# MLP second product: gate and residual applied to finished row blocks, first contributions copied by ScalarE

## The chip, the cores and the metric

The kernel runs on one core of a Trainium2 chip. The metric is the device time of one execution in microseconds (us). The engines are TensorE (PE, with its weight loads PEld), VectorE (DVE), ScalarE (ACT), GpSimd (POOL) and SyncE (SP), whose queue issues every DMA of this kernel. SBUF is the working memory of 128 partitions, PSUM the memory that TensorE writes its products to.

## The reference

One decoder layer over 2048 rows of width 1024, in float32. The last third is what matters here:

```
x = layer_norm(ALPHA * x + gt1 * y, ln1_g, ln1_b)
h = x * (1.0 + sc2) + sh2
f = square(relu(h @ w_ff1)) @ w_ff2          # 1024 -> 4096 -> 1024
x = layer_norm(ALPHA * x + gt2 * f, ln2_g, ln2_b)
```

`gt2` is one row of 1024 numbers (the gate), so `gt2 * f` scales the columns of `f`. `ALPHA * x` is the residual of the MLP.

## The kernel before

A scheduler orders the instructions of each engine when the program is built; on the chip every engine works through its own queue in that fixed order and waits where an input is late. Products in float32 are made of three passes over a high and a low part of each operand: `split` writes the high part with ScalarE and the low part (`x - high`) with VectorE, mostly; `mm3` issues three matmuls.

The stages that the change touches, with their place in the profile:

- **Output projection** (about 1080 to 1300 us). For each of 16 row tiles of 128 rows, `z` is normalised by ScalarE; then GpSimd makes `x2 = z * ag1 + ab1` in two instructions of 128x1024 (L1003, L1004), where `ag1` and `ab1` are ALPHA times the gain and bias of the first norm. `x2`, the residual, is stored to HBM (`ax2_d`).
- **First product** (about 1290 to 2002 us). Two halves of 1024 rows, 16 column blocks each. `split_h` makes seven operands of a half (Strassen's seven products P1 to P7; h, hh, hl in the profile; L1058 are its subtractions, on VectorE and GpSimd). In between, `prep` prepares `w_ff2` for the second product 16 times: load, multiply by the gate (two VectorE instructions of 128x1024, L1129), differences, split into w2s, store to `wt_d`.
- **Second product** (about 2002 us to the end). `down(half, s)` runs for two halves and four slices `s` of the inner dimension, seven products of 48 matmuls each. A half has eight row tiles, `acc[0]` to `acc[7]`. Before, `acc[t]` is loaded with the residual `x2` and every product is added to it by VectorE from PSUM (L1252). The products accumulate in PSUM banks W, Z and X (d_W, d_Z, d_X).
- **`finish(half, t)`** makes the second layer norm of a row tile: statistics (VectorE), 1/std (GpSimd, in `rs`), normalise (ScalarE), times `g2` (GpSimd), plus `b2` (GpSimd or VectorE), store. In the second half tiles 3, 5, 6 and 7 do it on VectorE alone with scalar_tensor_tensor (L1191, L1194). The eight `finish` of the first half run beside the first slice of the second half; those of the second half are the end of the program. In the last slice the order of products is P1, P5, P6, P3, P2, P7, P4; tiles 0 to 3 are finished after P2, tiles 4 to 7 after P4.

Of the kernel before, what the change touches and what calls it, by code (L numbers as in the profile page):

```python
# [10 lines left out]
F32 = mybir.dt.float32  # L11
# [105 lines left out]
def build(nc, tc, I, out, upto=9, dbg=None):  # L117
# [17 lines left out]
    ax2_d = tc.dram_tile((NT, P, D), F32, name="ax2_d")  # L135
# [12 lines left out]
    dbg.update(ax2=ax2_d, h=h_d, mix=mix_d, h2=h2_d, qn=qn_d, qr=qr_d, kn=kn_d, kr=kr_d, v=v_d, gt=gt_d)  # L148
# [785 lines left out]
    c3b = pool(p3, "c3b")  # L934
# [21 lines left out]
    ag0, ab0, ag1, ab1 = (p.tile([P, D], F32, name=n) for p, n in ((c3, "ag0"), (c3, "ab0"), (c3b, "ag1"), (c3b, "ab1")))  # L956
    for t, n in ((ag0, "ln_in_g"), (ab0, "ln_in_b"), (ag1, "ln1_g"), (ab1, "ln1_b")):
        rowbc(t, I[n])
        G.tensor_scalar(t, t, ALPHA, 0.0, op0=OP.mult, op1=OP.add)
# [12 lines left out]
    for b in border:  # L972
        xns = []
        for tp in range(2):
# [149 lines left out]
    def prep(u):  # L1124
# [3 lines left out]
        for i in range(2):  # L1128
            V.tensor_tensor(b[:, i], b[:, i], gt2, op=OP.mult)  # L1129
# [47 lines left out]
    g2 = c4.tile([P, D], F32, name="g2")  # L1177
    b2 = c4.tile([P, D], F32, name="b2")
    rowbc(g2, I["ln2_g"])
    rowbc(b2, I["ln2_b"])  # L1180
# [22 lines left out]
    def down(half, s, n):  # L1203
# [13 lines left out]
        def prod(x, name, ch, start, src, subs, *adds):  # L1217
# [62 lines left out]
    def load_acc(half, t):  # L1280
        acc[t] = acs[t].tile([P, D], F32, tag="c", name=f"acc{half}_{t}")
        with tc.issue_after(wdma[-1]):
            Q.dma_start(acc[t], ax2_d[4 * border[2 * half + t // 4] + t % 4])
# [56 lines left out]
```

## Time and profile before

| | |
|---|---|
| Three runs | 2644.70, 2646.72, 2647.34 us; median 2646.72 |
| The profiled execution | 2645.24 us, of which the span from first to last instruction is 2643.5 us and 1.7 us lie around it |
| Busy, share of the span | PE 93%, PEld 77%, DVE 68%, ACT 45%, POOL 43% |
| Granted TensorE clock, mean | 0.97 of 2.4 GHz |

A busy share is an average over stages with different limits; what a change is worth in one stage is read from that stage. A matmul of 128x512 starts 0.226 us after the one before it where TensorE runs without a gap at full clock (220 us held 972 of them between 2370 and 2590 us), so the count of matmuls in a stretch tells how much of it TensorE lost, be it by waiting or by a lower clock.

### The profile page before, as it was taken

How to read it: one execution, taken by the hardware profiler on the slowest of the kernel's cores; microseconds unless marked ns; L12 is line 12 of the kernel's file. 1: busy time of each engine (PE TensorE's matmuls, PEld its weight loads, DVE VectorE, ACT ScalarE, POOL GpSimd, SP SyncE). 2: the span in 40 equal slices, each digit the busy share in tenths (PEclk: the TensorE clock that was granted, in tenths of full speed). 3: DMA queues.
4: the chain of work that ended last, by engine and by line, in shares of the span. 5: the costliest groups of instructions: out<-in, count | busy, mean ns of one | idle time of the engine just before them, and what ended most of it. 6: DMA issues, size and time to landing. Idle time of an engine off the chain costs nothing.

```text
span 2643.5 us, 33756 instructions
## 1 busy us (share of the span) xinstructions
PE 2457.8 (93%) x11668; PEld 2028.1 (77%) x11668; DVE 1809.5 (68%) x2919; ACT 1188.1 (45%) x2317; POOL 1126.6 (43%) x1055
## 2 busy tenths in 40 slices
PE   6999999989999999899789999799999999999997
PEld 5887778877787878677577778677788888878885
DVE  8757675565767676766887755978645665776657
ACT  4653222246777777433455555455553111221111
POOL 4323545547978888577722223532220000330004
PEclk9999999988999999999889999899999999999998
DMA  9456341021112020655278863578838766776653
GB/s 327 146 196 224 108 133 50 31 73 32 48 37 61 20 62 13 219 183 192 104 263 268 280 229 107 174 255 278 293 123 349 271 245 256 295 301 244 225 191 127
DMA packets 194251, 464.69 MB, mean 176 GB/s; under 512 B 17560, under 2 KB 51736, under 8 KB 179744
## 3 DMA queue, kind: packets, MB, share of 16 engines
q1 hardware_dynamic: 194080, 462.54, 50.3%
q8 instruction: 92, 1.51, 0.2%
q14 instruction: 79, 0.65, 0.1%
HBM read 313.30 MB, written 149.17 MB: 175 GB/s over the span
## 4 chain that ended last, share of the span: by engine, by line
PE 54%; DVE 16%; DMA 13%; issue 6%; POOL 6%; ACT 5%; SPq 1%; DVEq 0%; ACTq 0%; POOLq 0%
DMA wt_d<-w2s 5%; PE d_W L131 4%; PE d_W L133 4%; PE d_W L132 4%; PE t L834 3%; DMA wad<-in_w_ada 2%; PE pj L133 2%; PE pj L132 2%; PE pj L131 2%; PE d_Z L132 2%; PE d_Z L133 2%; PE d_Z L131 2%; PE o L827 2%; PE o L825 2%; PE s L131 2%
## 5 line engine op out<-in xcount | busy, mean ns | idle before, releaser
L180 POOL TENSOR_SCALAR rs<-mv 128x1 f32<-128x1 f32 x32 | 16.0, 503 | 607.4 <-DVE mv L190 607.0
L128 DVE TENSOR_TENSOR w1l_P<-w,w1h_P 128x512 fp32r<-128x512 f32 x224 | 187.7, 844 | 69.4 <-ACT w1h_P L125 68.8
L806 ACT ACTIVATE p<-s,nm 128x512 f32<-128x512 f32 (+3 forms) x320 | 196.4, 627 | 41.8 <-DVE nm L803 38.3
L801 DVE TENSOR_REDUCE mx<-s 128x1 f32<-128x512 f32 (+3 forms) x288 | 175.0, 619 | 55.9 <-PE s L133 53.1
L1074 POOL TENSOR_TENSOR w<-w 128x512 f32<-128x512 f32 x56 | 81.7, 1463 | 286.7 <-DMA w<-in_w_ff 214.6
L125 ACT ACTIVATE w1h_P<-w 128x512 fp32r<-128x512 f32 x224 | 136.9, 622 | 108.2 <-PE u_Y L132 26.8
L850 POOL TENSOR_TENSOR tl<-tf,th 128x512 fp32r<-128x512 f32 x144 | 184.4, 1292 | 1.7
L834 PE MATMUL t<-ident,p 128*128 128x128 f32 x1088 | 164.3, 276 | 5.6 <-ACT tf L845 1.9
L834 PEld LDWEIGHTS t<-ident,p 128*128 128x128 f32 x1088 | 130.6, 142 | 30.8 <-ACT tf L845 6.1
L131 PE MATMUL pj<-wbh,hhb 128*128 128x512 f32 x384 | 151.3, 396 | 0.9 <-ACT wbh L125 0.5
L133 PE MATMUL pj<-wbh,hlb 128*128 128x512 f32 x384 | 152.1, 397 | 0.0
L132 PE MATMUL pj<-wbl,hhb 128*128 128x512 f32 x384 | 151.9, 396 | 0.2 <-DVE wbl L128 0.2
L131 PE MATMUL s<-kt,qt 96*128 96x512 f32 (+3 forms) x320 | 130.4, 408 | 11.5 <-ACT p L806 9.7
L1074 POOL TENSOR_TENSOR w<-w,w 128x512 f32<-128x512 f32 x56 | 81.8, 1461 | 133.8 <-DVE w1l_P L128 132.2
L128 DVE TENSOR_TENSOR w2s<-w2r,w2s 128x512 fp32r<-128x512 f32 x112 | 92.1, 825 | 66.8 <-ACT w2s L125 66.5
L125 ACT ACTIVATE w2s<-w2r 128x512 fp32r<-128x512 f32 x112 | 70.2, 628 | 146.0 <-DMA wt_d<-w2s 123.0
L827 PE MATMUL o<-tl,v 128*128 128x512 f32 (+2 forms) x320 | 123.3, 394 | 7.1 <-DVE tl L128 4.8
L825 PE MATMUL o<-th,v 128*128 128x512 f32 (+2 forms) x320 | 121.9, 385 | 5.6 <-DVE osum L861 4.5
L132 PE MATMUL s<-kt,qt 96*128 96x512 f32 (+3 forms) x320 | 120.4, 376 | 3.7 <-DVE kt L128 3.7
L133 PE MATMUL s<-kt,qt 96*128 96x512 f32 (+3 forms) x320 | 120.1, 376 | 0.0
L131 PE MATMUL u_W<-hh_P,w1h_P 128*128 128x512 f32 x256 | 102.6, 401 | 15.8 <-ACT hh_P L125 6.5
L133 PE MATMUL u_X<-hh_P,w1l_P 128*128 128x512 f32 x256 | 104.1, 408 | 12.4 <-DVE w1l_P L128 12.3
(372 smaller groups left out, 7850.6 us busy)
## 6 DMA issues: line engine op xcount, KB each, us to landing
wP<-wt_d SPq DMA_DIRECT2D x112, 1024.0 KB, 4.8
wt_d<-w2s SPq DMA_DIRECT2D x112, 512.0 KB, 4.9
w<-in_w_ff SPq DMA_DIRECT2D x64, 512.0 KB, 5.2
a<-g_d SPq DMA_DIRECT2D x32, 1024.0 KB, 6.3
g_d<-v SPq DMA_DIRECT2D x96, 256.0 KB, 4.2
wad<-in_w_ada SPq DMA_DIRECT2D x64, 256.0 KB, 2.9
w2r<-in_w_ff SPq DMA_DIRECT2D x16, 1024.0 KB, 7.7
x<-in_x SPq DMA_DIRECT2D x16, 512.0 KB, 8.2
```

What stands on the lines that cost most here:

```text
L125: A.activation(hi, x, AF.Copy)
L128: lo_eng.tensor_tensor(lo, x, hi.bitcast(F32), op=OP.subtract)
L131: T.matmul(ps, sh, mh, start=start, stop=False, skip_group_check=more)
L132: T.matmul(ps, sh, ml, start=False, stop=False, skip_group_check=more)
L133: T.matmul(ps, sl, mh, start=False, stop=stop, skip_group_check=more)
L801: V.tensor_reduce(mx[:, j:j + 1], ps[:, :n], op=OP.max, axis=AX.X)
L806: A.activation(pt[:, :m], b[:, :m], AF.Exp, bias=nm, accum_out=rs[:, qi, j:j + 1])
L825: T.matmul(po[:, cs], w, th[:, cs], start=(done == 0), stop=False)
L827: T.matmul(po[:, cs], w, tl[:, cs], start=False, stop=(done == nk))
L834: T.transpose(tp[:, qi * P:(qi + 1) * P], pts[h, 4 * qb + qi, kb // 4][1][:, kb % 4 * P:(kb % 4 + 1) * P], ident)
L850: (V if mode == "C" else G).tensor_tensor(tl[:, cs], tf[:, cs], th[:, cs].bitcast(F32), op=OP.subtract)
L1074: (V if half == 0 and c < W1V else G).tensor_tensor(src, *sub, op=op)
```

## The change

- `prep` no longer multiplies `w_ff2` by the gate. The gate and the residual are applied when a row tile is complete: `gate` multiplies `acc[t]` by `gt2` and adds the residual `zt`, two VectorE instructions of 128x1024 a tile.
- The output projection stores `z` itself (to `z_d`) and leaves out L1003 and L1004. `residual` loads `z` again for each of the 16 tiles, into a pool `ztp` of two slots, and GpSimd makes `z * ag1 + ab1` there, two instructions of 128x1024 a tile.
- With no residual in it at the start, `acc[t]` is no longer loaded. Its first contributions (P1, P5, P6 and P4 of slice 0) are written by ScalarE copies from PSUM; 32 VectorE adds and 16 loads go.
- In the last slice of the second half the gate of tiles 4 to 7 comes ahead of P4, and P4's own part is gated apart: `y = W * gt2`, `acc += y`, two VectorE instructions of 128x512 a tile. `y` takes a slot of `ztp`.
- `acc[0]` to `acc[3]` have one buffer in place of two. `gt2`, `ag1`, `ab1`, `g2` and `b2` are loaded in the second product, after slice 1.

```diff
-                    x2 = x3.tile([P, D], F32, tag="x2", name=f"x2_{tt}")
-                    G.tensor_tensor(x2, z, ag1, op=OP.mult)
-                    G.tensor_tensor(x2, x2, ab1, op=OP.add)
-                    Q.dma_start(ax2_d[tt], x2)
+                    Q.dma_start(z_d[tt], z)
...
-        for i in range(2):
-            V.tensor_tensor(b[:, i], b[:, i], gt2, op=OP.mult)
...
-    acs = [pool(p4b, f"ac{t}", 2) for t in range(8)]
+    acs = [pool(p4b, f"ac{t}", 1 if t < 4 else 2) for t in range(8)]
...
+    ztp = pool(p4b, "ztp", 2)
...
+    def residual(half, t):
+        zt = ztp.tile([P, D], F32, tag="zt", name=f"zt{half}_{t}")
+        with tc.issue_after(wdma[-1]):
+            Q.dma_start(zt, z_d[4 * border[2 * half + t // 4] + t % 4])
+        G.tensor_tensor(zt, zt, ag1, op=OP.mult)
+        G.tensor_tensor(zt, zt, ab1, op=OP.add)
+        return zt
+
+    def gate(f, zt):
+        V.tensor_tensor(f, f, gt2, op=OP.mult)
+        V.tensor_tensor(f, f, zt, op=OP.add)
 
     def finish(half, t):
         tt = 4 * border[2 * half + t // 4] + t % 4
         f = acc[t]
+        if half == 0 or t < 4:
+            gate(f, residual(half, t))
...
             if half == 1 and last and name == "P4":
                 ops = [parts(q) for q in range(2)]
                 for tp in range(4):
+                    gate(acc[4 + tp], residual(half, 4 + tp))
+                for tp in range(4):
                     for k in range(4):
                         mm(tp, k, *ops[k // 2])
+                    y = ztp.tile([P, D], F32, tag="zt", name=f"y{tp}")[:, 0:512]
+                    V.tensor_tensor(y, ps[ch, tp], gt2[:, 0:512], op=OP.mult)
+                    V.tensor_tensor(acc[4 + tp][:, 0:512], acc[4 + tp][:, 0:512], y, op=OP.add)
+                return
...
                     if s == 0 and name in ("P1", "P5"):
-                        load_acc(half, 4 * i + tp)
+                        acc[4 * i + tp] = acs[4 * i + tp].tile([P, D], F32, tag="c", name=f"acc{half}_{4 * i + tp}")
                     c = acc[4 * i + tp][:, 512 * j:512 * j + 512]
-                    V.tensor_tensor(c, c, ps[ch, tp], op=OP.add)
+                    if s == 0 and name in ("P1", "P5", "P6", "P4"):
+                        A.activation(c, ps[ch, tp], AF.Copy)
+                    else:
+                        V.tensor_tensor(c, c, ps[ch, tp], op=OP.add)
```

**GpSimd's queue at the start of the first product.** `h4_0_01` and `h4_0_00` are operands of `split_h`, `x2_2` and `x2_3` the residuals of the last two row tiles. Before:

```order
L1003 TENSOR_TENSOR x2_2_14679<-z2_14577,ag1_13258 128x1024
L1058 TENSOR_TENSOR h4_0_01_14849<-h4_0_11_14851,h4_0_01_14849 128x1024
L1004 TENSOR_TENSOR x2_2_14679<-x2_2_14679,ab1_13259 128x1024
L1003 TENSOR_TENSOR x2_3_14720<-z3_14589,ag1_13258 128x1024
L1058 TENSOR_TENSOR h4_0_00_14847<-h4_0_01_14849,h4_0_00_14847 128x1024
L1004 TENSOR_TENSOR x2_3_14720<-x2_3_14720,ab1_13259 128x1024
L1058 TENSOR_TENSOR h4_0_01_14849<-h4_0_10_14853,h4_0_01_14849 128x1024
L128 TENSOR_TENSOR hl0_P2_14886<-h4_0_10_14853,hh0_P2_14885 128x1024
```

And of the changed kernel, the same place:

```order
L1051 TENSOR_TENSOR h4_0_01_14786<-h4_0_11_14788,h4_0_01_14786 128x1024
L1051 TENSOR_TENSOR h4_0_00_14784<-h4_0_01_14786,h4_0_00_14784 128x1024
L1051 TENSOR_TENSOR h4_0_01_14786<-h4_0_10_14790,h4_0_01_14786 128x1024
L128 TENSOR_TENSOR hl0_P7_14815<-h4_0_00_14784,hh0_P7_14814 128x1024
L128 TENSOR_TENSOR hl0_P2_14823<-h4_0_10_14790,hh0_P2_14822 128x1024
```

The three subtractions stand one behind the other; the four residual instructions among and ahead of them are gone.

**VectorE's queue where the first half is finished** (after P2 of its last slice; gP7l and gP4l are low parts that TensorE waits for). Before:

```order
L1252 TENSOR_TENSOR acc0_0_20392<-acc0_0_20392,d0_3_X0_22044 128x512
L188 BN_STATS st_22112<-acc0_0_20392 128x6
L188 BN_STATS st_22126<-acc0_1_20395 128x6
L190 BN_AGGR mv_22115<-st_22112 128x2
L199 TENSOR_SCALAR nm_22118<-mv_22115,rs_22117 128x1
L128 TENSOR_TENSOR gP7l0_3_1_22201<-a4_0_3_00_21764,gP7h0_3_1_22200 128x1024
L1252 TENSOR_TENSOR acc0_1_20395<-acc0_1_20395,d0_3_X1_22045 128x512
```

Of the changed kernel:

```order
L1187 TENSOR_TENSOR acc0_2_20305<-acc0_2_20305,gt2_20224 128x1024
L128 TENSOR_TENSOR gP4l0_3_0_22167<-a4_0_3_11_21674,gP4h0_3_0_22166 128x1024
L1188 TENSOR_TENSOR acc0_1_20303<-acc0_1_20303,zt0_1_22040 128x1024
L1187 TENSOR_TENSOR acc0_3_20307<-acc0_3_20307,gt2_20224 128x1024
L1188 TENSOR_TENSOR acc0_2_20305<-acc0_2_20305,zt0_2_22060 128x1024
```

Between the low parts stand a multiplication by `gt2` and an addition of `zt` for each tile, and the addition waits for GpSimd's `zt`.

**GpSimd's queue at the end of the program**, from the norm of tile 1 of the second half. Before:

```order
L1199 TENSOR_TENSOR acc1_1_22427<-acc1_1_22427,g2_20316 128x1024
L1199 TENSOR_TENSOR acc1_2_22430<-acc1_2_22430,g2_20316 128x1024
L1200 TENSOR_TENSOR acc1_2_22430<-acc1_2_22430,b2_20317 128x1024
L180 TENSOR_SCALAR rs_24333<-mv_24331 128x1
L181 TENSOR_TENSOR rs_24333<-rs_24333,mhalf_115 128x1
```

Of the changed kernel:

```order
L1182 TENSOR_TENSOR zt1_5_24254<-zt1_5_24254,ag1_20225 128x1024
L180 TENSOR_SCALAR rs4_24163<-mv_24161 128x1
L1183 TENSOR_TENSOR zt1_5_24254<-zt1_5_24254,ab1_20226 128x1024
L181 TENSOR_TENSOR rs4_24163<-rs4_24163,mhalf_115 128x1
L1209 TENSOR_TENSOR acc1_1_22382<-acc1_1_22382,g2_20227 128x1024
L1209 TENSOR_TENSOR acc1_2_22384<-acc1_2_22384,g2_20227 128x1024
L1182 TENSOR_TENSOR zt1_6_24260<-zt1_6_24260,ag1_20225 128x1024
L1182 TENSOR_TENSOR zt1_7_24266<-zt1_7_24266,ag1_20225 128x1024
L1210 TENSOR_TENSOR acc1_2_22384<-acc1_2_22384,b2_20228 128x1024
L1183 TENSOR_TENSOR zt1_6_24260<-zt1_6_24260,ab1_20226 128x1024
L1183 TENSOR_TENSOR zt1_7_24266<-zt1_7_24266,ab1_20226 128x1024
```

The residuals of tiles 5 to 7 stand among the norms of tiles 1 and 2; `zt1_7` is the last of them.

## Rows read from the trace of the kernel before

**Rows 1.** The page: busy us, share of the span, instructions of two engines.
```profile
PE 2457.8 (93%) x11668; PEld 2028.1 (77%) x11668; DVE 1809.5 (68%) x2919; ACT 1188.1 (45%) x2317; POOL 1126.6 (43%) x1055
```

**Rows 2.** Stretches: length, busy PE, PEld, DVE, ACT, POOL (count), clock, DMA share, GB/s.
```profile
1290.00:1340.00 50.00, 27.57 (x90) 20.75 (x89) 41.94 (x34) 24.04 (x30) 34.71 (x15) 0.66 0.36 132
1340.00:1640.00 300.00, 284.14 (x1207) 229.37 (x1206) 206.10 (x284) 163.76 (x288) 72.05 (x51) 0.98 0.70 233
1640.00:1705.00 65.00, 51.37 (x193) 39.62 (x192) 62.76 (x46) 33.08 (x50) 43.97 (x18) 0.87 0.43 138
1705.00:2000.00 295.00, 283.56 (x1217) 228.92 (x1216) 199.56 (x270) 162.37 (x285) 78.88 (x55) 0.99 0.70 237
2270.00:2370.00 100.00, 93.69 (x404) 76.44 (x403) 83.64 (x95) 26.80 (x25) 43.82 (x28) 0.98 0.83 313
2370.00:2590.00 220.00, 220.00 (x972) 182.19 (x971) 131.43 (x147) 43.54 (x41) 0.00 (x0) 1.00 0.60 221
2590.00:2644.00 54.00, 33.68 (x138) 27.02 (x136) 44.45 (x60) 8.17 (x7) 27.47 (x23) 0.84 0.30 115
```

**Rows 3.** What PE waited for, 1290 to 1345 us: total, times, longest.
```profile
PE u_Y L132 <- DVE hl_P L128: 10.0, 2, 7.3
PE u_W L131 <- ACT hh_P L125: 6.5, 1, 6.5
```

**Rows 4.** GpSimd in order of time, 1290 to 1345 us: start, length, instruction.
```profile
1299.20 2.38 POOL L1003 TENSOR_TENSOR x<-z,ag 128x1024 f32<-128x1024 f32 x1
...
1318.80 2.37 POOL L1058 TENSOR_TENSOR h<-h,h 128x1024 f32<-128x1024 f32 x1 [2.35 <-issue]
```

**Rows 5.** VectorE at the second `split_h`: two gate multiplications in a row.
```profile
1681.59 5.65 DVE L1129 TENSOR_TENSOR w2r<-w2r,gt 128x1024 f32<-128x1024 f32 x2
```

**Rows 6.** ScalarE at the same place: idle time before the instruction, in brackets.
```profile
1685.05 0.63 ACT L125 ACTIVATE w2s<-w2r 128x512 fp32r<-128x512 f32 x1 [6.04 <-DVE w2r L1129]
```

**Rows 7.** All gate multiplications of `prep`: duration ns min/median/max, first and last.
```profile
L1129 DVE TENSOR_TENSOR w2r<-w2r,gt x32: 1211/1218/3423, 1333.4 to 1815.6; 128x1024 f32<-128x1024 f32 x32
```

**Rows 8.** What ScalarE waited for, 1330 to 1900 us.
```profile
ACT w2s L125 <- DMA wt_d<-w2s: 123.0, 67, 5.3
```

**Rows 9.** Adds from PSUM and statistics on `acc`: duration ns min/median/max.
```profile
L1252 DVE TENSOR_TENSOR acc<-acc,d_W x128: 628/686/690, 2011.9 to 2633.6; 128x512 f32<-128x512 f32 x128
L188 DVE BATCH_NORM_STATS2 st<-acc x32: 636/680/695, 2274.3 to 2634.3; 128x6 f32<-128x512 f32 x32
```

**Rows 10.** VectorE where the first half is finished, in order of time.
```profile
2277.77 0.69 DVE L1252 TENSOR_TENSOR acc<-acc,d_X 128x512 f32<-128x512 f32 x1 [0.47 <-PE d_X L133]
...
2297.10 3.41 DVE L1200 TENSOR_TENSOR acc<-acc,b 128x1024 f32<-128x1024 f32 x1 [0.35 <-POOL acc L1199]
...
2322.63 1.87 DVE L188 BATCH_NORM_STATS2 st<-acc 128x6 f32<-128x512 f32 x3
2324.42 1.20 DVE L1200 TENSOR_TENSOR acc<-acc,b 128x1024 f32<-128x1024 f32 x1
2325.54 1.21 DVE L1223 TENSOR_TENSOR a<-a,a 128x1024 f32<-128x1024 f32 x1
...
2366.31 1.23 DVE L128 TENSOR_TENSOR gP2l<-a,gP2h 128x1024 fp32r<-128x1024 f32 x1 [4.21 <-ACT gP2h L125]
```

**Rows 11.** GpSimd at the same place.
```profile
2282.46 2.40 POOL L1199 TENSOR_TENSOR acc<-acc,g 128x1024 f32<-128x1024 f32 x1 [1.61 <-ACT acc L1198]
...
2294.64 8.12 POOL L1199 TENSOR_TENSOR acc<-acc,g 128x1024 f32<-128x1024 f32 x3
```

**Rows 12.** VectorE at the end of the program: first and last instruction.
```profile
2591.20 0.69 DVE L1252 TENSOR_TENSOR acc<-acc,d_X 128x512 f32<-128x512 f32 x1 [0.47 <-PE d_X L133]
...
2638.98 1.41 DVE L1194 SCALAR_TENSOR_TENSOR acc<-acc,rs,b 128x512 f32<-128x512 f32 x2
```

**Rows 13.** DMA issues: KB each, median us from issue to landing.
```profile
axl<-in_x SPq DMA_DIRECT2D x16, 512.0 KB, 4.4
```

**Rows 14.** A ScalarE copy from PSUM: duration ns min/median/max.
```profile
L1100 ACT ACTIVATE u<-u_X x31: 574/578/587, 1337.9 to 1986.7; 128x512 f32<-128x512 f32 x31
```

More of the change, by code (lines that the diff above doesn't have):

```diff
@@ L133, in mm3 @@
         T.matmul(ps, sl, mh, start=False, stop=stop, skip_group_check=more)
-    ax2_d = tc.dram_tile((NT, P, D), F32, name="ax2_d")
+    z_d = tc.dram_tile((NT, P, D), F32, name="z_d")
     h_d = [tc.dram_tile((4, P, KD, P), F32, name=f"h_d{b}") for b in range(NB)]
@@ L147, in build @@
     gt_d = [tc.dram_tile((1, D), F32, name=f"gt_d{i}") for i in range(2)]
-    dbg.update(ax2=ax2_d, h=h_d, mix=mix_d, h2=h2_d, qn=qn_d, qr=qr_d, kn=kn_d, kr=kr_d, v=v_d, gt=gt_d)
+    dbg.update(z=z_d, h=h_d, mix=mix_d, h2=h2_d, qn=qn_d, qr=qr_d, kn=kn_d, kr=kr_d, v=v_d, gt=gt_d)
     ctx = ExitStack()
@@ L933, in build @@
     x3 = pool(p3, "x3", 2)
-    c3b = pool(p3, "c3b")
     sm3 = pool(p3, "sm3", 4)
@@ L955, in build @@
                 split(t, *wo[n][k], A, WL[n])
-    ag0, ab0, ag1, ab1 = (p.tile([P, D], F32, name=n) for p, n in ((c3, "ag0"), (c3, "ab0"), (c3b, "ag1"), (c3b, "ab1")))
-    for t, n in ((ag0, "ln_in_g"), (ab0, "ln_in_b"), (ag1, "ln1_g"), (ab1, "ln1_b")):
+    ag0, ab0 = (c3.tile([P, D], F32, name=n) for n in ("ag0", "ab0"))
+    for t, n in ((ag0, "ln_in_g"), (ab0, "ln_in_b")):
         rowbc(t, I[n])
@@ L1024, in build @@
     psf = [pool(p4, f"psf{i}", 4, space=PSUM) for i in range(2)]
-    gt2p = pool(p4, "gt2p", side="right")
-    gt2 = gt2p.tile([P, D], F32, name="gt2")
-    rowbc(gt2, gt_d[1])
     p4a = p4.enter_context(ExitStack())
@@ L1166, in build @@
     raws = [pool(p4b, f"raw{i}") for i in range(4)]
-    acs = [pool(p4b, f"ac{t}", 2) for t in range(8)]
-    raws += [pool(p4b, f"raw{i}") for i in range(4, 7)]
+    acs = [pool(p4b, f"ac{t}", 1 if t < 4 else 2) for t in range(8)]
+    raws += [pool(p4b, f"raw{i}") for i in range(4, 8)]
     gp = pool(p4b, "gp", GB)
     wl = pool(p4b, "wl", WLB)
-    raws.append(pool(p4b, "raw7"))
     c4 = pool(p4b, "c4")
+    ztp = pool(p4b, "ztp", 2)
     sm4 = pool(p4b, "sm4", 4)
@@ L1176, in build, with load_rows @@
     wdma = []
[L1177 to L1180, printed above, removed]
+    gt2, ag1, ab1, g2, b2 = (c4.tile([P, D], F32, name=n) for n in ("gt2", "ag1", "ab1", "g2", "b2"))
+    rows = (gt2, gt_d[1]), (ag1, I["ln1_g"]), (ab1, I["ln1_b"]), (g2, I["ln2_g"]), (b2, I["ln2_b"])
+    def load_rows():
+        with tc.issue_after(wdma[-1]):
+            for t, src in rows:
+                rowbc(t, src)
+        for t in (ag1, ab1):
+            G.tensor_scalar(t, t, ALPHA, 0.0, op0=OP.mult, op1=OP.add)
+    def residual(half, t):
+        zt = ztp.tile([P, D], F32, tag="zt", name=f"zt{half}_{t}")
+        with tc.issue_after(wdma[-1]):
+            Q.dma_start(zt, z_d[4 * border[2 * half + t // 4] + t % 4])
[5 more added lines that the diff above has]
+        V.tensor_tensor(f, f, zt, op=OP.add)
     def finish(half, t):
@@ L1278, in down @@
                 finish(half, 4 + tp)
[L1280 to L1283, printed above, removed]
     for half in range(2):
@@ L1287, in build @@
             down(half, s, half * NST + s)
+            if half == 0 and s == 1:
+                load_rows()
     p4.close()
```

## The prediction

> **What bounds the kernel now.** The page comes first: TensorE is busy 93% of the span, VectorE 68% and GpSimd 43% [rows 1], so the question is where TensorE is not fed. The stretches answer it by the count of matmuls. At full clock 220 us hold 972 of them, one every 0.226 us [rows 2]. By that measure TensorE lost about 29 us between 1290 and 1340 (90 in place of 221), 27 between 1340 and 1640, 21 between 1640 and 1705, 20 between 1705 and 2000, and 9 between 2270 and 2370; from 2370 to 2590 it lost nothing [rows 2]. The second product is thus bound by TensorE but for two places: where the first half is finished beside the next half's first products (2270 to 2370), and the end.
>
> The second thing to see is what VectorE and GpSimd do to each other. A VectorE instruction of 128x1024 with both inputs in SBUF takes 1.20 us alone, and one starts 1.12 us after the other in a queue; beside three GpSimd instructions in a row it took 3.41 us [rows 10, 11]. That is the 2.40 us of a GpSimd instruction [rows 11] plus its own time: one waits for the other, in both directions. Adds from PSUM and statistics are not held: none of them took over 0.69 us [rows 9].
>
> These two places can be priced as a plain sum: VectorE's two-input work at 1.13 us, adds and statistics at 0.62 (three in 1.87 us [rows 10]), a scalar_tensor_tensor of 512 at 0.70 (two in 1.41 [rows 12]), and GpSimd's large instructions at 2.40, one behind the other. From the first add of X in the first half's last P2 (2277.77) to the second low part of the next half's P2 (2367.54) VectorE's queue holds 27 two-input instructions, 28 adds and 15 statistics, GpSimd 12 large ones: 30.5 + 26.7 + 28.8 = 86 us; measured 89.8 [rows 10]. At the end, from 2591.20 to 2640.39, it holds 4, 12, 15, 16 scalar_tensor_tensor and 7 GpSimd ones: 4.5 + 16.7 + 11.2 + 16.8 = 49 us; measured 49.2 [rows 12]. In both, the two engines hardly gained by being two.
>
> **The change part by part.**
>
> *Gains ahead of the second product.* GpSimd loses the 32 residual instructions of the output projection. At the start of the first product two pairs of them stand among the three subtractions that feed TensorE's low parts: the first starts at 1299.20, and the third subtraction only at 1318.80 [rows 4]. Without the four, at least 2.4 us each, that subtraction comes some 10 to 14 us earlier, and VectorE beside it is held less. TensorE waited 10.0 us for hl and 6.5 us for hh there [rows 3] and lost 29 us in all with its clock at 0.66 [rows 2]. I take 11 us, bounds 5 and 18. In the output projection itself I take 4 us for VectorE and the norms being held less, bounds 0 and 8.
>
> The 32 gate multiplications of `prep` take 1.2 us of VectorE each, up to 3.4 [rows 7]. At the second `split_h` two of them took 5.65 us [rows 5] and ScalarE stood 6.04 us for them [rows 6], with w1h of the running product behind; 5 us of the 21 come back. In the other preps ScalarE waits for the stores of w2s to land, 123 us in 67 waits [rows 8]; the change leaves that chain as it is, so of the 47 us that TensorE lost there I take 7, bounds 0 and 12. Sum of gains 27 us, bounds 9 and 43.
>
> *Costing nothing.* The 32 adds that ScalarE takes over as copies cost it 0.58 us each [rows 14]; ScalarE has 27 us of work in the 100 us from 2270 [rows 2], so the time is hidden. Its queue is not quite: with one buffer for `acc[0]` to `acc[3]` the copy of the next half waits until the finished tile has been stored, and P6's high part stands behind it. I leave that inside the bounds below. The 16 loads of `acc` become 16 loads of `zt`. The adds removed in the first half's slice 0 lie beside a TensorE that has nothing to wait for.
>
> *Cost where the first half is finished.* VectorE's queue from the same add to the same low part now holds 43 two-input instructions (16 more: two for each of eight tiles), 16 adds (12 fewer) and 16 statistics; GpSimd has 24 large ones in place of 12 (16 for `zt`, of which the first four can be done before the stretch begins, because tiles 0 and 1 find both slots free). The plain sum is 48.6 + 19.8 + 57.6 = 126 us, 40 more than before. The lower bound lets adds and statistics run beside GpSimd for nothing: 48.6 + 57.6 = 106 us, 16 more than the measured 89.8. VectorE was already late for TensorE there, so what this stretch grows by is lost. Going down both queues row by row with the durations above I get 15 to 20 us at the next half's P3, because here VectorE also waits for TensorE and ScalarE, and GpSimd uses that; I take 20.
>
> *Cost at the end.* VectorE's 4 two-input instructions become 20, and four more of 512 read `y`; GpSimd's 7 become 19. The plain sum is 22.6 + 19.8 (12 adds, 16 statistics, 4 of `y`) + 11.2 + 45.6 = 99 us, 50 more. The lower bound, without adds and statistics, is 22.6 + 2.5 + 11.2 + 45.6 = 82 us, 33 more than 49.2. Here nothing else is going on, and the two slots of `ztp` make a chain: an addition frees a slot, the load lands 4.4 us later (the like load of the output projection [rows 13]), GpSimd needs two instructions for it, each held by one of VectorE, and behind it the order puts the norms of tiles 1 and 2 as well. Going down the queues, the additions of `zt` for tiles 2, 3, 5 and 7 end 24, 39, 51 and 73 us after the start, and 21 us of statistics, `y` and scalar_tensor_tensor are left: 94 us, 45 more than before. I take 44. P4 on TensorE starts some 5 us later than before, and that is not what ends last.
>
> *Sum.* 20 + 44 - 27 = 37 us more than the profiled execution's 2645.2, which lies 1.5 us below the median of the runs: 2682 against that execution, 2684 as a median.
>
> **Rivals.**
>
> *The residual is ready in time* (other side). If GpSimd's `zt` were done in VectorE's gaps and no addition waited for it, VectorE's own instructions alone would count: at the end 16 x 1.13 + 4 x 0.62 + 0.6 = 21 us; where the first half is finished 18 us come and 7 go, which TensorE's slack may take. 2645 + 21 - 27 = 2639. It decides at whether a third residual can be ready when the second is used; there are two slots, and the sums of before show no such overlap. Chance 0.10.
>
> *The relief ahead of the second product is larger.* Were all that TensorE lost between 1290 and 2000 given back (97 us) and the 64 lost again, 2645 - 33 = 2612; half of it gives 2661. Against it stand the 123 us of waits for stores, which stay. That it outweighs the cost: 0.05.
>
> *Only the two-input work excludes itself.* If adds from PSUM and statistics run beside GpSimd for nothing, both places come out at their lower bounds: 16 + 33 - 27 = 22 us, 2667 (2669 as a median). For it speaks that these instructions were never held, at most 0.69 us [rows 9]; against it, that before the two places took the full sum none the less. Chance 0.25. The Trainium skill, SBUF — State Buffer, section "Who interferes with whom", states that rule: a VectorE instruction with two SBUF inputs and a GpSimd instruction reading SBUF exclude each other, whoever starts first, and one with at most one SBUF input does not contend. By that rule the time is this rival's; the trace agrees on which instructions are held (3.41 us against at most 0.69).
>
> *VectorE and GpSimd add up fully, and the gains fail.* 40 + 50 - 9 = 81 us: 2727. For it speaks that the sums of before fit without overlap. At this end or beyond, over 2714: 0.10.
>
> *The gate leaves `prep` and nothing comes of it.* If the waits for stores set the pace of all preps, 12 us of the gains go: 2696. Chance 0.10; my forecast, with what lies closer to it than to any rival, has 0.40.
>
> **How the numbers follow.** The range goes from 2652 (lower bounds of both costs, 49, and gains of 43) to 2714 (costs 40 + 50 with gains of 21). It leaves out the two faster cases and the end beyond. Three runs of before spread by 0.1%; a change under 0.2% (5 us) can't be told from none. Faster 0.11, the same 0.04, slower 0.85, all from the cases above.
>
> **What would show it.** Right: in the profile after, VectorE's additions of `zt` and its low parts of P4 to P6 take over 2 us where the first half is finished, and that stretch holds 30 to 60 fewer matmuls than unhindered; from the last add of X for tile 0 to the last instruction pass 85 to 100 us, with VectorE waiting for `zt` of tiles 6 and 7; the start of the first product holds clearly more than 90 matmuls in the like 50 us. The prediction is wrong if `zt` is waited for nowhere, if GpSimd's instructions stay at 2.4 us with VectorE's at 1.2, or if the first product is shorter by more than 45 us.

## The result, and the profile after

The changed kernel takes 2684.9 us (median of 4 runs, 2679.95 to 2685.61) beside 2645.71 us for the kernel before (2642.19 to 2647.34): ratio 1.0146, 95% interval 1.0128 to 1.0164, or 39 us slower. The profiled execution after took 2684.99 us, with a span of 2683.2.

To see where the time went, the span of each profiled execution is cut at four instructions that both kernels have: the first matmul of the output projection (`psY`), of the first product (`u_X`), of the second product (`d_W` from `gP1h`), and the last one of that third group, in the last slice. These rows give, before and then after, count, duration in ns (min/median/max) and first and last start in us:

```profile
L131 PE MATMUL psY<-wo_h,mh x256: 387/389/774, 1082.3 to 1288.0; 128*128 128x512 f32 x128
L131 PE MATMUL u_X<-hh_P,w1h_P x256: 388/389/632, 1289.5 to 1996.1; 128*128 128x512 f32 x128
L131 PE MATMUL d_W<-wP,gP1h x128: 389/389/500, 2002.7 to 2555.0; 128*128 128x512 f32 x128
```

```profile
L131 PE MATMUL psY<-wo_h,mh x256: 387/389/792, 1077.8 to 1271.4; 128*128 128x512 f32 x128
L131 PE MATMUL u_X<-hh_P,w1h_P x256: 388/389/796, 1272.8 to 1973.0; 128*128 128x512 f32 x128
L131 PE MATMUL d_W<-wP,gP1h x128: 389/389/504, 1979.6 to 2553.1; 128*128 128x512 f32 x128
```

| stage, us | before | after | difference |
|---|---|---|---|
| all ahead of the output projection | 1082.3 | 1077.8 | -4.5 |
| output projection | 207.2 | 195.0 | -12.2 |
| first product | 713.2 | 706.8 | -6.4 |
| second product up to its last slice (first half finished in it) | 552.3 | 573.5 | +21.2 |
| last slice and the end | 88.5 | 130.1 | +41.6 |

The first row can't be told from scatter: four kernels run below that differ from the changed kernel only behind that point (x1_raw, x3_vec, x4_slots, x7_vcopy) begin the output projection between 1074.4 and 1081.2 us. The other four rows add up to +44.

**Where the first half is finished.** The stretches of after (columns as in [rows 2]) that answer to those of before, shifted by the earlier start of each stage:

```profile
1272.00:1322.00 50.00, 30.97 (x117) 23.68 (x116) 41.16 (x43) 26.73 (x36) 19.85 (x10) 0.80 0.49 167
1322.00:1613.00 291.00, 275.60 (x1174) 221.38 (x1173) 191.02 (x259) 158.98 (x278) 73.63 (x51) 0.98 0.71 233
1613.00:1680.00 67.00, 54.39 (x211) 42.58 (x210) 62.49 (x52) 36.24 (x56) 41.69 (x17) 0.90 0.44 137
1680.00:1980.00 300.00, 286.24 (x1226) 229.86 (x1225) 188.58 (x252) 165.69 (x287) 79.84 (x56) 0.99 0.69 234
2247.00:2347.00 100.00, 78.24 (x310) 61.63 (x309) 94.55 (x78) 23.42 (x28) 75.44 (x35) 0.91 0.60 215
2588.00:2683.20 95.20, 33.91 (x138) 27.21 (x137) 86.27 (x81) 7.99 (x7) 63.34 (x35) 0.69 0.27 99
```

From 2247 to 2347 TensorE does 310 matmuls where it did 404: 94 x 0.226 = 21 us, the whole growth of this stage. VectorE is busy for 94.6 of 100 us (83.6 before), GpSimd for 75.4 (43.8 before). VectorE and then GpSimd in order of time there, excerpts; "x2" is two in a row:

```profile
2288.41 3.42 DVE L1187 TENSOR_TENSOR acc<-acc,gt 128x1024 f32<-128x1024 f32 x1
2291.75 0.20 DVE L199 TENSOR_SCALAR nm<-mv,rs 128x1 f32<-128x1 f32 x1
2291.88 6.63 DVE L1233 TENSOR_TENSOR a<-a,a 128x1024 f32<-128x1024 f32 x2
```

```profile
2287.62 3.13 POOL L1182 TENSOR_TENSOR zt<-zt,ag 128x1024 f32<-128x1024 f32 x1
2290.82 3.27 POOL L1183 TENSOR_TENSOR zt<-zt,ab 128x1024 f32<-128x1024 f32 x1
2294.05 3.38 POOL L1209 TENSOR_TENSOR acc<-acc,g 128x1024 f32<-128x1024 f32 x1
```

Line the two up: three GpSimd instructions pass between 2287.6 and 2297.4, and three of VectorE's between 2288.4 and 2298.5. Each of either engine takes about 3.35 us, 2.4 plus 1.2 less an overlap of a quarter of a microsecond, so both advance in step. The two `a` sums held up here (`a + a`, L1233) feed the next half's P5, and TensorE later stands for its low part, as for those of P1 and P6. What it waited for from 2247 to 2347 (us in total, times, longest):

```profile
PE d_W L133 <- DVE gP6l L128: 7.3, 2, 5.6
PE d_Z L133 <- DVE gP5l L128: 5.3, 1, 5.3
PE d_W L131 <- DVE acc L1271: 4.4, 1, 4.4
PE d_W L133 <- DVE gP1l L128: 2.5, 1, 2.5
PE d_W L131 <- ACT acc L1269: 1.2, 1, 1.2
PE d_W L131 <- ACT gP1h L125: 1.0, 1, 1.0
```

These waits are 21.7 us; before, from 2270 to 2370, they were 6.3. They are thus 15 of the 21 us. The granted clock fell too, from 0.98 to 0.91: behind the wait of 4.4 us a dozen matmuls start 0.43 us apart in place of 0.226, the lower of the clock's two levels (1.2 and 2.4 GHz).

**The end.** VectorE's additions of `zt`, from the first X addition to its last instruction:

```profile
2589.38 0.69 DVE L1271 TENSOR_TENSOR acc<-acc,d_X 128x512 f32<-128x512 f32 x1 [0.37 <-PE d_X L133]
...
2606.00 3.42 DVE L1188 TENSOR_TENSOR acc<-acc,zt 128x1024 f32<-128x1024 f32 x1
...
2610.47 1.21 DVE L1188 TENSOR_TENSOR acc<-acc,zt 128x1024 f32<-128x1024 f32 x1
...
2623.05 1.21 DVE L1188 TENSOR_TENSOR acc<-acc,zt 128x1024 f32<-128x1024 f32 x1
...
2637.19 3.35 DVE L1188 TENSOR_TENSOR acc<-acc,zt 128x1024 f32<-128x1024 f32 x1
...
2653.84 3.34 DVE L1188 TENSOR_TENSOR acc<-acc,zt 128x1024 f32<-128x1024 f32 x1 [4.53 <-POOL zt L1183]
...
2658.62 1.22 DVE L1188 TENSOR_TENSOR acc<-acc,zt 128x1024 f32<-128x1024 f32 x1
...
2678.72 1.40 DVE L1204 SCALAR_TENSOR_TENSOR acc<-acc,rs,b 128x512 f32<-128x512 f32 x2
```

It takes 90.7 us where it took 49.2 [rows 12], and VectorE stands still for `zt` only once, 4.5 us before the seventh tile; all its idle time there is 5.5 us, as much as before. The rest of the growth is VectorE instructions that run or are held: in the last of the stretches above VectorE is busy 86.3 of 95.2 us and GpSimd 63.3, where before it was 44.5 and 27.5 of 54 [rows 2]. All instructions of a kind after, duration ns min/median/max:

```profile
L1187 DVE TENSOR_TENSOR acc<-acc,gt x16: 1210/1943/3418, 2255.4 to 2625.3; 128x1024 f32<-128x1024 f32 x16
L1188 DVE TENSOR_TENSOR acc<-acc,zt x16: 1166/1226/3416, 2256.7 to 2658.6; 128x1024 f32<-128x1024 f32 x16
L1182 POOL TENSOR_TENSOR zt<-zt,ag x16: 2335/2599/3382, 2241.8 to 2645.4; 128x1024 f32<-128x1024 f32 x16
L1271 DVE TENSOR_TENSOR acc<-acc,d_W x100: 623/686/689, 2032.3 to 2617.0; 128x512 f32<-128x512 f32 x100
L188 DVE BATCH_NORM_STATS2 st<-acc x32: 633/676/695, 2258.0 to 2667.3; 128x6 f32<-128x512 f32 x32
```

As in [rows 9], additions from PSUM and statistics are never held; instructions with two SBUF inputs take up to 3.42 us.

**The output projection.** Its gain shows on one VectorE instruction, the addition of `ab0`, which has two SBUF inputs; before and after:

```profile
L987 DVE TENSOR_TENSOR axl<-axl,ab x16: 1206/3407/3424, 1104.1 to 1277.2; 128x1024 f32<-128x1024 f32 x16
```

```profile
L986 DVE TENSOR_TENSOR axl<-axl,ab x16: 1209/1226/3400, 1097.4 to 1259.1; 128x1024 f32<-128x1024 f32 x16
```

TensorE's largest wait of before in this stage is gone after, and VectorE, which hardly ever had to wait for the products of `psY`, now does (us in total, times, longest; one line of TensorE before, then VectorE's before and after):

```profile
PE psT L965 <- ACT h2f L967: 7.9, 5, 2.9
```

```profile
DVE z L997 <- PE psY L133: 0.5, 1, 0.5
```

```profile
DVE z L996 <- PE psY L133: 23.8, 14, 4.0
```

GpSimd's own queue was late there as well. In the chain of work that ended last, from 1082 to 1290 us of before, GpSimd's multiplication of `axl` and the two residual instructions have 29% of the time and VectorE's addition 9%; in after, from 1078 to 1273, the matmuls of `psY` have 73%.

**The first product.** TensorE's start gains: 117 matmuls in its first 50 us against 90 [rows 2], 27 x 0.226 = 6.1 us, at a granted clock of 0.80 instead of 0.66. The wait of 6.5 us for `hh` is gone. Those for `hl` come to 11.1 us, where before they were 15.3 (10.0 in [rows 3], 3.8 for `u_Z` and 1.5 for `u_W`), and waits for parts of `w1` are new. All waits of TensorE from 1272 to 1328 us after:

```profile
PE u_Y L132 <- DVE hl_P L128: 5.4, 1, 5.4
PE u_X L131 <- ACT w1h_P L125: 4.4, 1, 4.4
PE u_Z L132 <- DVE hl_P L128: 4.0, 1, 4.0
PE u_X L133 <- DVE w1l_P L128: 3.5, 1, 3.5
PE u_W L132 <- DVE hl_P L128: 1.7, 1, 1.7
```

The rest of this product gains next to nothing: at 0.226 us a matmul the three stretches from 1322 to 1980 lost 26, 19 and 23 us, those of before 27, 21 and 20. In the preps ScalarE still waits for stores of `w2s`, here from 1315 to 1885 us; before it was 123.0 us [rows 8]:

```profile
ACT w2s L125 <- DMA wt_d<-w2s: 107.4, 56, 6.3
```

and at the second `split_h`, where it waited 6.04 us for two gate multiplications [rows 6], it now waits 3.31 and 2.52 us for the subtractions that stood behind them:

```profile
1661.25 0.63 ACT L125 ACTIVATE w2s<-w2r 128x512 fp32r<-128x512 f32 x1 [3.31 <-DVE w2r L1125]
...
1667.43 0.63 ACT L125 ACTIVATE w2s<-w2r 128x512 fp32r<-128x512 f32 x1 [2.52 <-DVE w2r L1125]
```

### The profile page after: what moved, and what is told of

The parts are those of the page before. It is cut to its first block, busy times and chain, and to the rows that moved or that the text cites. A ratio compares the mean times of both kernels' runs of the same rounds, so it can differ in the third digit from the quotient of the medians.

```text
span 2683.2 us, 33774 instructions
## 1 busy us (share of the span) xinstructions
PE 2451.4 (91%) x11668; PEld 2022.3 (75%) x11668; DVE 1815.8 (68%) x2891; ACT 1204.9 (45%) x2349; POOL 1135.9 (42%) x1055
## 4 chain that ended last, share of the span: by engine, by line
PE 60%; DVE 16%; DMA 11%; issue 5%; ACT 4%; POOL 4%; SPq 0%; DVEq 0%; ACTq 0%; POOLq 0%
DMA wt_d<-w2s 5%; PE d_W L131 4%; PE d_W L132 4%; PE d_W L133 4%; PE t L834 3%; DMA wad<-in_w_ada 2%; PE d_Z L133 2%; PE d_Z L132 2%; PE d_Z L131 2%; PE pj L133 2%; PE pj L131 2%; PE pj L132 2%; PE o L827 2%; PE o L825 2%; PE s L131 2%
## 5 line engine op out<-in xcount | busy, mean ns | idle before, releaser
L128 DVE TENSOR_TENSOR w1l_P<-w,w1h_P 128x512 fp32r<-128x512 f32 x224 | 195.4, 875 | 79.2 <-ACT w1h_P L125 78.0
L1182 POOL TENSOR_TENSOR zt<-zt,ag 128x1024 f32<-128x1024 f32 x16 | 44.4, 2784 | 350.8 <-DMA zt<-z_d 350.8
L834 PEld LDWEIGHTS t<-ident,p 128*128 128x128 f32 x1088 | 130.1, 142 | 29.8 <-ACT tf L845 6.1
L125 ACT ACTIVATE w2s<-w2r 128x512 fp32r<-128x512 f32 x112 | 70.2, 626 | 120.3 <-DMA wt_d<-w2s 107.4
L131 PE MATMUL u_X<-hh_P,w1h_P 128*128 128x512 f32 x256 | 105.5, 412 | 19.8 <-ACT w1h_P L125 17.0
```

The lines of the kernel that those rows point to most:

```text
L125: A.activation(hi, x, AF.Copy)
L128: lo_eng.tensor_tensor(lo, x, hi.bitcast(F32), op=OP.subtract)
L131: T.matmul(ps, sh, mh, start=start, stop=False, skip_group_check=more)
L834: T.transpose(tp[:, qi * P:(qi + 1) * P], pts[h, 4 * qb + qi, kb // 4][1][:, kb % 4 * P:(kb % 4 + 1) * P], ident)
```

## The experiments

The theory: where VectorE has more to do than TensorE leaves it time for, its two-input instructions and GpSimd's large ones take turns, so each GpSimd instruction there costs its 2.4 us; where TensorE or a DMA sets the pace it costs nothing. The rivals: VectorE's own new instructions are the cost; or the chain through the two slots of `ztp` is. The kernels of one group of runs share their runs of the kernel before: 2641.75 us for the first four, 2643.14 for the next four, 2643.27 for the last two; kernels of different groups are therefore compared by their ratios to it. Each variant is scheduled anew, so its queues can differ from those of the changed kernel in order too; no run separates that. All stages, cut as above, each from one profiled execution ("OP" is the output projection):

| kernel | ahead | OP | first product | second, to last slice | end | time us | ratio to before, interval |
|---|---|---|---|---|---|---|---|
| before | 1082.3 | 207.2 | 713.2 | 552.3 | 88.5 | 2645.7 | |
| after | 1077.8 | 195.0 | 706.8 | 573.5 | 130.1 | 2684.9 | 1.0146, 1.0128 to 1.0164 |
| x1_raw | 1074.4 | 195.9 | 706.4 | 557.0 | 109.4 | 2646.7 | 1.0023, 1.0013 to 1.0034 |
| x2_early | 1078.5 | 206.7 | 710.0 | 558.6 | 109.4 | 2663.7 | 1.0084, 1.0068 to 1.0100 |
| x3_vec | 1078.3 | 195.0 | 707.3 | 561.5 | 119.4 | 2664.5 | 1.0087, 1.0066 to 1.0107 |
| x4_slots | 1081.2 | 193.7 | 704.7 | 574.5 | 127.8 | 2681.7 | 1.0152, 1.0135 to 1.0170 |
| x5_nogate | 1078.1 | 205.8 | 711.1 | 553.9 | 88.6 | 2635.6 | 0.9977, 0.9965 to 0.9989 |
| x6_noscale | 1078.6 | 193.9 | 708.3 | 553.9 | 88.5 | 2625.3 | 0.9929, 0.9915 to 0.9942 |
| x7_vcopy | 1077.3 | 195.4 | 705.2 | 583.3 | 130.0 | 2694.8 | 1.0191, 1.0177 to 1.0205 |
| c1_spread | 1079.8 | 196.6 | 708.5 | 546.4 | 89.0 | 2618.0 | 0.9900, 0.9885 to 0.9915 |
| c2_vend | 1074.1 | 196.3 | 705.7 | 546.5 | 84.0 | 2611.9 | 0.9883, 0.9866 to 0.9901 |
| c3_vboth | 1078.6 | 193.9 | 708.1 | 543.4 | 84.0 | 2609.8 | 0.9872, 0.9854 to 0.9890 |

**x1_raw: GpSimd's part of the finishing work left out.**

```diff
         Q.dma_start(zt, z_d[4 * border[2 * half + t // 4] + t % 4])
-        G.tensor_tensor(zt, zt, ag1, op=OP.mult)
-        G.tensor_tensor(zt, zt, ab1, op=OP.add)
         return zt
```

> The changed kernel without GpSimd's two instructions on each residual tile: the row block is added as it was loaded, so the scaling by ag1 and the addition of ab1 are left out. VectorE keeps all that it has.
> Theory (VectorE's two-input instructions and GpSimd's large ones exclude each other, so at both finishing places the two engines' work adds up): GpSimd's residual work is most of the cost. At the end the plain sum falls from 99 to 70 us, so the end comes 20 to 25 us earlier; at the half boundary 8 to 16 us come back. Time 2644 to 2657 us, and VectorE's gate and residual instructions take 1.2 us in the mean instead of 1.9 and 2.3.
> Rival A (VectorE's own new instructions are the cost): nothing of VectorE's is taken away, so the time stays above 2672 us.
> Rival B (the two slots of ztp and the load's latency set the pace): the slots are still two and each load still follows the addition that frees its slot; 2665 to 2685 us.

2646.7 us; by the ratios (1.0023 and 1.0146) 33 us less than after. In the traces the stage with the half boundary is 16.5 us shorter, the end 20.7. VectorE's gate and residual instructions, all still there, take a median of 1.21 us:

```profile
L1185 DVE TENSOR_TENSOR acc<-acc,gt x16: 1164/1212/2826, 2252.5 to 2601.2; 128x1024 f32<-128x1024 f32 x16
L1186 DVE TENSOR_TENSOR acc<-acc,zt x16: 1165/1212/3354, 2253.7 to 2615.3; 128x1024 f32<-128x1024 f32 x16
```

So of the 62.8 us that the two places cost in the traces, 37.2 go with GpSimd's 32 instructions and 25.6 (4.7 and 20.9) stay with the rest of the change, VectorE's new instructions above all. At the end rival A holds for half of the cost; alone it would have left all of it.

**x2_early: the residual made in the output projection again.** To x1_raw are added the two rows, their scaling, and

```diff
+                    x2 = x3.tile([P, D], F32, tag="x2", name=f"x2_{tt}")
+                    G.tensor_tensor(x2, z, ag1, op=OP.mult)
+                    G.tensor_tensor(x2, x2, ab1, op=OP.add)
+                    Q.dma_start(ax2_d[tt], x2)
-                    Q.dma_start(z_d[tt], z)
```

> The changed kernel with the residual made in the output projection again, as in the kernel before, and only loaded where a row block is finished. Against the kernel without GpSimd's two instructions the only difference is where GpSimd's 32 instructions stand.
> Theory (the 17 us that the output projection gained came from the 32 GpSimd instructions leaving it): 12 to 17 us longer than the kernel that adds the raw row; about 2655 to 2672 us. The second product starts 8 to 17 us later than in the changed kernel.
> Rival (the gain ahead of the second product comes from the gate leaving prep, or from the two row loads alone): within 5 us of the kernel that adds the raw row, 2644 to 2660 us, and the second product starts within 5 us of the changed kernel's 1979.6.

2663.7 us, 17 more than x1_raw in the same runs. In the traces 10.8 us of that lie in the output projection, 3.6 in the first product, whose start the last of these instructions reach, and 1.6 in the stage with the half boundary; the end is as in x1_raw. Another 4.1 lie ahead of the output projection, within the scatter of that point.

**x3_vec: the residual's two instructions on VectorE.**

```diff
-        G.tensor_tensor(zt, zt, ag1, op=OP.mult)
-        G.tensor_tensor(zt, zt, ab1, op=OP.add)
+        V.tensor_tensor(zt, zt, ag1, op=OP.mult)
+        V.tensor_tensor(zt, zt, ab1, op=OP.add)
```

> The changed kernel with the two residual instructions of each tile on VectorE in place of GpSimd. Nothing is left out; VectorE gets 32 more two-input instructions, GpSimd loses 32.
> Theory (the two engines take turns, so only the sum counts): a two-input instruction of 128x1024 costs 1.13 us of the turn on VectorE and 2.4 on GpSimd. At the end 12 of GpSimd's at 2.4 become 16 of VectorE's at 1.13, 11 us less; at the half boundary the same and up to 11 us less. Time 2660 to 2674 us: less although the fuller engine gets more.
> Rival A (VectorE is the bound at both places and its own count decides): 16 instructions of 1.13 us more at each place, less the 4.5 us for which VectorE waited for zt at the end: 2705 to 2717 us.
> Rival B (the chain of two slots): loads, two instructions and the addition follow one another as before, with shorter instructions; 2670 to 2690 us.

2664.5 us: by the ratios (1.0087 and 1.0146) 16 us less than after, although VectorE, the busier of the two, got 32 instructions more. In the traces the half boundary is 12.0 us cheaper, the end 10.7. This is the run that tells most: had VectorE's count alone decided, the time would have risen by 20 us or more. With less of GpSimd beside it the added instructions cost 1.2 us each, and so does most of the rest:

```profile
L1183 DVE TENSOR_TENSOR zt<-zt,ab x16: 1165/1212/2001, 2246.4 to 2639.3; 128x1024 f32<-128x1024 f32 x16
L1187 DVE TENSOR_TENSOR acc<-acc,gt x16: 1166/1215/3418, 2256.4 to 2610.5; 128x1024 f32<-128x1024 f32 x16
```

**x4_slots: four slots for `zt`.**

```diff
-    ztp = pool(p4b, "ztp", 2)
+    ztp = pool(p4b, "ztp", 4)
...
-        G.tensor_tensor(zt, zt, ag1, op=OP.mult)
-        G.tensor_tensor(zt, zt, ab1, op=OP.add)
+        G.tensor_tensor(zt, zt, g2, op=OP.mult)
+        G.tensor_tensor(zt, zt, b2, op=OP.add)
```

The loads of `ag1` and `ab1` and their scaling are left out with it.

> The changed kernel with four slots for zt in place of two. It reads g2 and b2 where the changed kernel reads ag1 and ab1, whose space the slots need, so the scaled rows of the first norm are left out; the instructions and their sizes are the same.
> Theory (the engines' turns are the cost): the work is the same and only 4.5 us of VectorE's time at the end is a wait for zt; 2676 to 2686 us.
> Rival B (the chain of two slots: an addition frees a slot, a load, two instructions, the next addition): with four slots two tiles more are ready ahead at each place, 10 us or more each: 2655 to 2668 us.

2681.7 us; its ratio and that of after can't be told apart. In the traces the end is 2.3 us shorter, the half boundary 1.0 longer. The slots are not the cause.

**x5_nogate and x6_noscale: each gain by itself, in the kernel before.** x5_nogate takes the gate out of `prep` and puts it nowhere; x6_noscale stores the normalised rows unscaled.

```diff
-        for i in range(2):
-            V.tensor_tensor(b[:, i], b[:, i], gt2, op=OP.mult)
```

> The kernel before without the 32 gate multiplications of prep; the gate of the MLP is left out altogether, all else is as before.
> Theory (the preps' pace is set by the stores of w2s; the gate matters only at the second split_h and a little elsewhere): 3 to 9 us less than before, 2633 to 2639 us beside a before of 2642; the first product alone is shorter by that.
> Rival (the gate in VectorE's queue is what holds up TensorE in each prep): 12 us less or more, at most 2630 us.

```diff
-                    G.tensor_tensor(x2, z, ag1, op=OP.mult)
-                    G.tensor_tensor(x2, x2, ab1, op=OP.add)
-                    Q.dma_start(ax2_d[tt], x2)
+                    Q.dma_start(ax2_d[tt], z)
```

> The kernel before with the 32 residual instructions of GpSimd left out of the output projection (the normalised rows are stored unscaled, so the scaling by ag1 and ab1 is left out) and with the two row loads gone.
> Theory (they and nothing else held up the output projection): 13 to 20 us less than before, 2622 to 2629 us beside 2642; the output projection ends 13 to 18 us earlier.
> Rival (half of what the changed kernel gained there came from other orders of loads): 4 to 9 us less.

x5_nogate: by the ratio 3 to 9 us less than before. In its trace only 2.1 us of that lie in the first product; 4.2 lie ahead of the output projection, where nothing was changed. Leaving the gate out of `prep` is thus worth 3 to 9 us by the runs and 2.1 in its own stage by the one trace; which of the two is nearer, the runs don't show. x6_noscale: 15 to 22 us less by the ratio; in its trace 13.3 in the output projection and 4.9 in the first product. Nearly all that the change gains in its trace (18.6 us in these two stages) is here.

**x7_vcopy: first contributions copied by VectorE.**

```diff
-                        A.activation(c, ps[ch, tp], AF.Copy)
+                        V.tensor_copy(c, ps[ch, tp])
```

> The changed kernel with the 32 copies of first contributions on VectorE in place of ScalarE. Nothing is left out.
> Theory (the copies are 0.6 us each; at the half boundary VectorE is late, ScalarE is not): 16 of them stand at the half boundary, 10 us of VectorE's time, of which GpSimd's turn hides some: 2 to 10 us more than the changed kernel, 2684 to 2694 us beside a before of 2642 and 2681 for the changed kernel.
> Rival (the copies on ScalarE, which wait there for a finished tile's store and stand ahead of the high parts, cost as much as they save): the same as the changed kernel or less, 2672 to 2683 us.

2694.8 us, ratio 0.0045 above that of after, 12 us; in the traces 9.8 us, all where the first half is finished. The next half's first slice has sixteen of these copies at 0.68 us, 11 us on the engine that is late: the copies on ScalarE are a part of the change that pays.

**c1_spread: gate left in `prep`, residual applied while VectorE has time.** On the changed kernel, with the gate in `prep` and out of `finish`, one slot for `zt`, one buffer for three tiles of `acc`, the rows loaded after slice 0, and in `prod` (cut):

```diff
+            t = {"P5": 0, "P3": 1, "P7": 2, "P4": 3}.get(name) if s in (1, 2) else None
+            if t is not None:
+                t += 4 * (s - 1)
+                zt = residual(half, t)
...
+            if t is not None:
+                V.tensor_tensor(acc[t], acc[t], zt, op=OP.add)
```

> The gate is applied in prep as in the kernel before. The residual is not applied where a row block is finished but in slices 1 and 2 of the second product, one row block beside each of four of the seven products: load, GpSimd's two instructions, VectorE's addition. First contributions are copied by ScalarE as in the changed kernel. Nothing is left out.
> Theory (GpSimd's large instructions cost only where VectorE is late already; in slices 1 and 2 VectorE has a third of its time free): the 13 to 17 us of the output projection stay won, the two finishing places cost what they cost before (the half boundary up to 5 us less, for its 12 fewer additions): 2620 to 2632 us beside a before of 2642.
> Rival (GpSimd's large instructions hold up VectorE, and through it TensorE, wherever they stand): 64 instructions more of either engine in slices 1 and 2 cost TensorE 10 us or more there: 2638 to 2655 us.

2618.0 us, 1.0% less than before. In the traces the output projection keeps 10.6 us, the first product 4.7, and the end is as it was. The stage with the half boundary is 5.9 us shorter, which goes with the copies on ScalarE (x7_vcopy has 9.8 us for them, in the changed kernel), though no run leaves them out of c1_spread. In slices 1 and 2 the moved work costs TensorE nothing: 842 matmuls in 190 us of the first half from 2060 us on, 842 before from 2078 on, and in the second half 620 against 619. The kernel before, then c1_spread, in 140 us of the second half's slices 1 and 2 (columns as in [rows 2]):

```profile
2385.00:2525.00 140.00, 140.00 (x619) 115.96 (x618) 85.57 (x94) 27.61 (x26) 0.00 (x0) 1.00 0.60 222
```

```profile
2365.00:2505.00 140.00, 140.00 (x620) 115.91 (x619) 97.72 (x97) 28.99 (x30) 33.55 (x13) 1.00 0.69 251
```

VectorE's busy time grows by 12 us with three instructions more, and it is held here as well (the `a` sums and differences take 1.48 us in the mean, 1.22 before); it had the time.

**c2_vend and c3_vboth: GpSimd's last norm work on VectorE.** On c1_spread, c2_vend for the second half, c3_vboth for both (shown):

```diff
-FB4 = "GVGVGVGV", "GVGVGVGV"
-FM4 = "GGGGGGGG", "GGGGGGGG"
+FB4 = "VVVVVVVV", "VVVVVVVV"
+FM4 = "VVVVVVVV", "VVVVVVVV"
```

> The kernel with the residual spread over slices 1 and 2 and the gate in prep, and besides at the end of the program VectorE in place of GpSimd for the last norm's scaling and addition of the four tiles that GpSimd shares there (0, 1, 2 and 4). Nothing is left out.
> Theory (turns): seven GpSimd instructions of 2.4 us at the end become seven of VectorE's of 1.13, 9 us less in the sum; in VectorE's queue they stand behind ScalarE's normalisation of each tile, which gives some of it back. 4 to 9 us less than the same kernel without it (2618 beside a before of 2643), 2609 to 2614 us.
> Rival (VectorE is the bound at the end and its own count decides): seven instructions more, 8 us more: 2626 us.

> The same, and also where the first half is finished: the last norm's scaling and addition of all eight tiles there on VectorE, 12 of them taken from GpSimd. Nothing is left out.
> Theory (turns): 12 instructions of 2.4 us become 12 of 1.13, 15 us less in the sum of that place; TensorE lost 9 us there in the kernel before, so at most that comes back: 2 to 9 us less than the kernel that does it at the end alone.
> Rival (here VectorE is late for TensorE and waits in order for ScalarE's normalisation, while GpSimd is not on the path): 12 instructions more in VectorE's queue, 5 to 14 us more than the kernel that does it at the end alone.

c2_vend: 2611.9 us, the end 5.0 us shorter in the trace (84.0, and 84.0 again in c3_vboth, against 88.5 to 89.0 in four kernels with GpSimd's work there); its interval overlaps that of c1_spread. c3_vboth: 2609.8 us, 1.3% less than before and the lowest median here; its half boundary is 3.1 us shorter in the trace, but the intervals of the two overlap, so the times don't tell it from c2_vend, and the 3.1 us rest on one trace of each. At neither place did the added VectorE instructions cost time.

## Why the prediction was right, and where its terms were not

**What bounds the kernel**: right. The places named as VectorE's bottlenecks are the two that grew, and x3_vec shows that there a GpSimd instruction costs more than the same work on VectorE; the traces of c2_vend and c3_vboth agree.

**Cost where the first half is finished**: 20 taken, 21.2 measured. One figure of "What would show it" does not fit its own term: 20 us are 88 matmuls, and the stretch lost 94 against before (132 against 442 unhindered), not 30 to 60. From the first add of X to the second low part of P2 VectorE took 114.4 us (2254.69 to 2369.11), between the bound of 106 and the plain sum of 126. That before the plain sum (86) came so near 89.8 was in part chance: VectorE stood still for 12.8 of these 89.8 us, so the engines did gain by being two; after, it stood still for 5.1 of 114.4. The sign that VectorE's instructions take over 2 us there came true for some of them: three of eight additions of `zt` took 3.4 us there, the others 1.2, and of the six low parts of P4 to P6 three took over 3.2 us.

**Cost at the end**: 44 taken, 41.6 measured. The walk down the queues said that the additions for tiles 2, 3, 5 and 7 end 24, 39, 51 and 73 us after the start and all ends at 94; the trace has 22, 35, 51, 70 and 90.7. The plain sum (99) is too high and the bound without additions and statistics (82) too low. The chain of two slots, which the walk has as a part of its pace, is not what sets it: four slots shortened the end by 2.3 us (x4_slots), and `zt` was waited for at tile 6 alone, not at 6 and 7. The Trainium skill, SBUF — State Buffer, section "Who interferes with whom", says which VectorE instructions exclude GpSimd's, and the rows of after agree (0.70 us at most for additions and statistics, 3.42 for two-input work). Going by its rule alone gave 2669, and the time came out higher, 2684.9. A likely reason, which no run tests, is that of two engines that each go through their queue in order, VectorE rarely has an addition from PSUM to run just when GpSimd holds the turn. In x1_raw, where GpSimd has seven large instructions left there, the end took 68.7 us (2569.95 to 2638.7), close to the plain sum, 99 - 12 x 2.4 = 70.

**Gains**: 27 taken, 18.6 measured in the traces (12.2 + 6.4), and not where they were expected. The step "in the output projection itself I take 4 us" was mis-sized: it is 12.2 (13.3 alone, in x6_noscale). The prediction had read no row on what sets that stage's pace. There `axl`'s addition was held in most cases (median 3407 ns), and VectorE waited for matmuls of `psY` 0.5 us in all; after, with its additions free, 23.8 us. GpSimd's queue was on the path as well, with 29% of the chain. x6_noscale shows that GpSimd's 32 instructions are the cause; whether they cost by holding VectorE or by filling GpSimd's own queue stays open. The start of the first product gave 6.1 of 11, within its bounds. "Of the 47 us ... I take 7" and the 5 of the second `split_h` came to little: the first product has 0.3 us beyond its start, and x5_nogate 2.1 in that stage (3 to 9 in all by its runs). At the second `split_h` the wait passed to the next instruction, and in the preps waits of 107.4 us for the stores of `w2s` stayed. The gains were thus 8.4 us too high and the costs 1.2; the 4.5 us ahead of the output projection, which no term has, took back most of the difference. A total of +37 against +39 is in part luck.

**Costing nothing**: the copies on ScalarE are hidden, as said. With one buffer, ScalarE did wait 10.0 us for two stores, and TensorE 1.2 us for ScalarE.

**The rivals.** A residual ready in time: `zt` was waited for only once, yet the cost came, since being ready is not what decides; the 21 us that this rival gave for VectorE's own instructions at the end are what x1_raw left there (20.9). Larger relief: no. Full addition: neither place reached its plain sum (114.4 of 126 and 90.7 of 99). That the gate's leaving `prep` gives nothing was nearly right in the traces; its 2696 was missed because the output projection gave more.

## What to carry to other kernels

Before work is moved from one engine to another, ask which engine is late in the stage where it lands, and price every large GpSimd instruction there as time taken from VectorE as well; a plain sum over both queues was within a tenth of the time at the end of this program. Where VectorE is late, the same two-input instruction on VectorE was cheaper than on GpSimd here, and work that may stand anywhere belongs where TensorE sets the pace: here the two GpSimd instructions a tile of the same residual cost 33 to 37 us at the finish, 14 to 18 in the output projection and the start of the first product, and nothing in the middle slices.

## What was not expected of the hardware

GpSimd's instructions on 128x1 can be drawn out as well: the scaling of `rs` takes 0.22 us in the median and up to 1.20 us, as long as a VectorE instruction; before:

```profile
L180 POOL TENSOR_SCALAR rs<-mv x32: 212/222/1201, 1114.5 to 2636.6; 128x1 f32<-128x1 f32 x32
```

And the place of a stage moves more than its length: the output projection begins at 1074.4 us in x1_raw and at 1081.2 in x4_slots, whose edits stand only behind it, and lasts 195.9 and 193.7 us.
